# A token mixer's issue order: the forgetting norm's chain at high priority, a split traced behind the first casts, the stick-breaking sums bound two tiles on

## The chip, the cores and the metric

The kernel runs on one core of one Trainium2 chip. The metric is device time in microseconds (us) for one execution of the whole program; lower is better. Five engines run side by side, each with its own instruction stream, and meet only through semaphores: PE (TensorE, with its weight loads listed apart as PEld), DVE (VectorE), ACT (ScalarE), POOL (GpSimd) and SP (SyncE, which here only issues DMAs).

## The reference

A decoder trunk of two layers over 256 tokens of width 1024, in float32. Each layer is a feed-forward block (SwiGLU), a token mixer, and a second feed-forward block, each behind an RMS norm with a shift, a scale and a gate computed from a conditioning vector. The change lies in the mixer alone:

```python
def _mixer(h, w_in, ...):
    proj = h @ w_in
    (lru_x, lru_g, sb_q, sb_k, sb_v, fx_q, fx_k, fx_v, fx_f) = jnp.split(proj, SPLIT_POINTS, axis=-1)
    u = _causal_depthwise_conv(lru_x, conv_w, conv_b)
    y_lru = _rg_lru(u, ...) * jax.nn.gelu(lru_g)                   # recurrence
    y_sb = _stick_breaking_attention(sb_q, sb_k, sb_v)             # weights exp(log_beta + sums of log_1mb)
    fq, fk = _rms(fx_q) * g_qk[0], _rms(fx_k) * g_qk[1]            # the forgetting norm
    log_f = jax.nn.log_sigmoid(fx_f + b_fgate)
    y_fox = _forgetting_attention(fq, fk, fx_v, log_f)
    y = jnp.concatenate([_rms(y_lru), _rms(y_sb), _rms(y_fox)], axis=-1) * g_mix_out
    return y @ w_out
```

## The kernel before, in words

Tokens are two tiles of 128 rows (`t` = 0, 1). Every large weight arrives as a unit of 128x1024 float32 values (`raw`, six buffers), and is split into two parts that a fast matmul takes: `H`, a rounded copy made by ACT (L251), and `L`, the rest `raw - H`, made by DVE (L253). The activations are split in the same way into `hTh` and `hTl`, eight feature tiles of 128 each. A product is three matmuls: H with hTh, L with hTh, H with hTl.

The order of the instructions on each engine isn't written by hand. A scheduler places them at build time by a model of their times: whenever an engine comes free in its model, it takes, of the instructions whose inputs are ready, the one with the lowest priority number, which is the place in the program. Two constructs bend this. `with tc.high_priority()` gives what it holds the priority of the start of the program. `with tc.issue_after(ins)`, here often through the helper `behind(mul)`, lets what it traces on the engine of `ins` be queued only behind `ins`; on other engines it does nothing. On the chip every engine then runs its queue in that order, whatever is ready.

The mixer (`mixer`) goes through these steps, per layer:

- `proj(g, t)` multiplies the normed activations by the columns of group `g`: LG and LX (gate and input of the recurrence), FX (the forgetting q and k), then `proj_w(SB, b)` (stick-breaking q and k), then VV (both values). Each `proj` result lies in one of two PSUM banks (`PA`), so the third is not begun before the first is read out. `muls[g, t]` keeps the last matmul of each of the eight feature tiles; `muls[VV, 1][4]` is that of tile 4 of VV for the second token tile.
- Recurrence: four taps (L688, L691), the gates `go` (L698) with sigmoid and tanh, then, after `load_table("natural_log_exp_and_others")`, exponentials, a scan (L778) and the product with the gate (L831).
- The forgetting norm's chain, for each `t` (L726 to L734): square of the projection `o` on ACT (`fsq`), a sum over each head on DVE (`s8`), two logarithms and one exponential on ACT (`r8`), and the product `qa = o * r8` on DVE (L734), which is the last reader of the bank that holds `o`.
- Softmax of the forgetting attention, with its weights `p0`, `p1`; they are transposed later (L913) and copied to `pa`, `pb` (L914).
- The recurrence's group norm `group(hs, ...)` (L853 is its last product), and right behind it, at L861, `split(0, 4, hs)`: for each of four feature tiles one ACT instruction that writes `hTh` (L821) and one DVE instruction that reads it and writes `hTl` (L822).
- The stick-breaking weights, for two halves `e` = 0, 1: logits `zb`, `za` in PSUM; on ACT an absolute value, exponential and logarithm; on DVE L887; then casts on ACT (L893, `gh` and `ah`) and the remainders on DVE (L894, `gl` and `al`); then the sums, six matmuls onto `zb` and `za` (called through `more`, L231), at high priority and behind a tile of VV; then two exponentials (`wsb`, `wsa`).
- `values` (L925), the two remaining group norms and splits (feature tiles 6, 7 and 4, 5), and the output projection `w_out` (L264 to L266), whose first four feature tiles are the recurrence's. Then residual, the next norm (`xn`, L413) and its transposes (`tp`, L424), and the next feed-forward block (L277).

The helper that the change calls a second time is this:

```python
        def split(f0, n, src):
            for i in range(n):
                g = gm[:, f0 + i:f0 + i + 1]
                yh, yl = hTh[:, :, f0 + i, :], hTl[:, :, f0 + i, :]
                y = src[:, i, :].rearrange("p (t q) -> p t q", t=NT)
                A.activation(yh, y, AF.Copy, scale=g)
                V.scalar_tensor_tensor(out=yl, in0=y, scalar=g, in1=yh.bitcast(F32), ...)
```

Of the kernel before, what the change touches and what calls it, by code (L numbers as in the profile page):

```python
# [13 lines left out]
AF = mybir.ActivationFunctionType  # L14
ALU = mybir.AluOpType
AX = mybir.AxisListType
# [12 lines left out]
HD = 64  # L29
LX, LG, SB, FX, VV = range(5)  # L30
# [64 lines left out]
def trunk_kernel(ctx: ExitStack, tc: tile.TileContext, x, c, wst, ada, par, cst, row, wg, out):  # L95
# [14 lines left out]
    def W4(shape, dt=F32, name="w4"):  # L110
        return w4.tile(shape, dt, tag="w4", name=name)

    def W2(shape, dt=F32, name="w2"):
        return w2.tile(shape, dt, tag="w2", name=name)

    def SM(shape, dt=F32, name="sm"):
        return sm.tile(shape, dt, tag="sm", name=name)
# [4 lines left out]
    def PD(shape, name):  # L122
        return psd.tile(shape, F32, tag="d", name=name)

    def PT(shape, name):
        return pst.tile(shape, F32, tag="t", name=name)

    V, A, T, S = nc.vector, nc.scalar, nc.tensor, nc.sync
# [35 lines left out]
    def C(name):  # L164
        o, n = CST[name]
        return c_sb[:, o:o + n]

    def R(name):
        o, n = ROW[name]
        return r_sb[:, o:o + n]  # L170
# [7 lines left out]
    for n in range(2):  # L178
        q = slice(n * 512, (n + 1) * 512)
        o = PT([128, 512], name="pc")  # L180
# [5 lines left out]
    eps_t = const.tile([128, 1], F32, name="eps_t")  # L186
    V.memset(eps_t, EPS)
    eps64_t = const.tile([128, 1], F32, name="eps64_t")
# [41 lines left out]
    def more(o, **k):  # L230
        T.matmul(o, start=False, stop=True, skip_group_check=True, **k)  # L231
# [234 lines left out]
    def act(*a, **k):  # L466
        with tc.issue_after(table[-1].ins) if table else nullcontext():
            used.append(A.activation(*a, **k))  # L468
        return used[-1]
# [148 lines left out]
    def mixer(l, after):  # L618
# [7 lines left out]
        muls = {}  # L626

        def proj(g, t):
            o = PA([128, 512], name="pj")

            def w(k):
                q = slice((k % 2) * 512, (k % 2 + 1) * 512)
                if (g, t) == (LX, 0) and k == 2:
                    rooted.append(1)
                return [part[:, q] for part in unit(("in", l, g, k // 2))]

            muls[g, t] = over_features(o, t, w, (K_T[2], flush) if (g, t) == (LX, 0) else None, by=1)
            rooted.clear()
            ada_step(ADA_MIX[l] if g in (FX, VV) else 0)
            return o  # L640

        def proj_w(g, b):

            o = PA([128, 2, SEQ], name="pj")
            with ExitStack() as behind:
                for k in range(KT):
                    wh, wl = unit(("in", l, g, k // 2))
                    for h, w in ((0, wh), (0, wl), (1, wh)):
                        for i in range(2):
                            q = (k % 2) * 512 + (2 * b + i) * 128  # L650
                            opens = k == 0 and h == 0 and w is wh and i == 0
                            mul = T.matmul(o[:, i], lhsT=w[:, q:q + 128], rhs=(hTh, hTl)[h][:, :, k, :], start=opens,  # L652
                                           stop=True, skip_group_check=True)
                            if opens:
                                behind.enter_context(tc.issue_after(mul.ins))
            ada_step(ADA_MIX[l])
            return o

        def behind(mul):
            return tc.issue_after(mul.ins)  # L660
# [24 lines left out]
        if True:  # L685
            for f2, hf in enumerate(halves):
                for f in (2 * f2, 2 * f2 + 1):
                    A.activation(u[:, f, :], xT[:, f, 3:3 + SEQ], AF.Identity,  # L688
                                 scale=cw[:, 3 * 4 + f:3 * 4 + f + 1], bias=cbias[:, f:f + 1])
# [4 lines left out]
                for gi, (dst, b) in enumerate(((rg, P(f"br{l}")), (ig, P(f"bi{l}")))):  # L694
                    o = PD([128, 2, SEQ], name="go")
# [10 lines left out]
        qa = [const.tile([128, 8, 66], F32, name=f"qa{t}", tag=f"qa{t}") for t in range(NT)]  # L706
        for t in range(NT):
            o = proj(FX, t)
            if t == 1:
                z4 = SM([128, NT, 4], name="z4")  # L710
                fo = PT([8, NT, 128], name="fo")
                with tc.high_priority(), behind(muls[FX, 1][2]):
                    for k in range(KT):
                        T.matmul(fo, lhsT=wfs[:, k, :], rhs=hTh[:, :, k, :], start=k == 0, stop=False)
                        T.matmul(fo, lhsT=wfs[:, k, :], rhs=hTl[:, :, k, :], start=False, stop=k == KT - 1)
                zs = W2([8, NT, 128], name="zs")
                A.copy(zs, fo)
                zo = PT([128, NT, 4], name="zo")
                with behind(muls[FX, 1][7]):
                    for i in range(NT):  # L720
                        T.matmul(zo[:, i, :], lhsT=zs[:, i, :], rhs=C("fold")[0:8, :], start=True, stop=True)
                V.tensor_tensor(out=z4, in0=zo, in1=R(f"bf{l}").unsqueeze(1).to_broadcast([128, NT, 4]), op=ALU.add)
                z4 = z4.rearrange("p t h -> p (t h)")
            o3 = o.rearrange("p (h d) -> p h d", d=HD)
            sq = W2([128, 8, HD], name="fsq")
            A.activation(sq, o3, AF.Square)  # L726
            s8 = SM([128, 8], name="s8")
            V.tensor_reduce(out=s8, in_=sq, axis=AX.X, op=ALU.add)

            r8 = SM([128, 8], name="r8")  # L730
            act(r8[:, 0:4], s8[:, 0:4], AF.Ln, bias=eps64_t)
            act(r8[:, 4:8], s8[:, 4:8], AF.Ln, scale=1.0 / HD, bias=eps_t)
            act(r8, r8, AF.Exp, scale=-0.5)
            V.tensor_tensor(out=qa[t][:, :, 0:HD], in0=o3,  # L734
                            in1=r8.unsqueeze(2).to_broadcast([128, 8, HD]), op=ALU.mult)
            for i in range(2):
                V.tensor_tensor(out=qa[t][:, 4 * i:4 * i + 4, 0:HD], in0=qa[t][:, 4 * i:4 * i + 4, 0:HD],
                                in1=R(f"gqk{l}")[:, i * HD:(i + 1) * HD].unsqueeze(1).to_broadcast([128, 4, HD]),
                                op=ALU.mult)
            V.memset(qa[t][:, 0:4, 65:66], 1.0)  # L740
            V.memset(qa[t][:, 4:8, 64:65], 1.0)
# [26 lines left out]
        hs = W4([128, 4, SEQ], name="hs")  # L768
# [39 lines left out]
        for b in range(2):  # L808
            o = proj_w(SB, b)
# [6 lines left out]
# [6 lines that stand above are left out]
                V.scalar_tensor_tensor(out=yl, in0=y, scalar=g, in1=yh.bitcast(F32),  # L822
                                       op0=ALU.mult, op1=ALU.subtract)
# [58 lines left out]
        for e in range(2):  # L882
            for z, n in ((zb[e], nb[:, e]), (za[e], na[:, e])):
                A.activation(n, z, AF.Abs)
                act(n, n, AF.Exp, scale=-1.0)
                act(n, n, AF.Ln, bias=1.0)
                V.scalar_tensor_tensor(out=n, in0=z, scalar=0.0, in1=n, op0=ALU.max, op1=ALU.add)  # L887

            parts = []
            part_b = [gtp.tile([128, 2, 128], F32R, tag=n, name=n) for n in ("gh", "gl")]  # L890
            part_a = [W2([128, 2, SEQ], F32R, name=n) for n in ("ah", "al")]
            for n, (h, lo) in ((nb[:, e], part_b), (na[:, e], part_a)):
                A.copy(h, n)  # L893
                V.tensor_tensor(out=lo, in0=n, in1=h.bitcast(F32), op=ALU.subtract)  # L894
                parts.append((h, lo))
            with tc.high_priority(), behind(muls[VV, 1][(2, 6)[e]]):
                for i in range(2):
                    more(zb[e], lhsT=ntri_r, rhs=parts[0][i])
                    more(za[e][:, :, 128:256], lhsT=nones_r, rhs=parts[0][i])
                for i in range(2):  # L900
                    more(za[e], lhsT=ntri_r, rhs=parts[1][i])
            act(wsb[:, e], zb[e], AF.Exp)
            act(wsa[:, e], za[e], AF.Exp)
# [33 lines left out]
        o = {}  # L937
# [84 lines left out]
    for l in range(DEPTH):  # L1022
        ffn(l, 0, norm(l, 1), pre if l == 0 else {})
        mixer(l, norm(l, 2))
        ffn(l, 1, norm(l + 1, 0) if l + 1 < DEPTH else None)
# [94 lines left out]
```

## Time and profile before

| what | value |
|---|---|
| time, median of 3 runs | 994.08 us (993.16 to 994.2) |
| the profiled execution's own time | 993.75 us |
| its span, from the first to the last instruction | 992.0 us |
| granted TensorE clock | 1.000 |
| ACT busy | 531.6 us (54%) |
| DVE busy | 761.4 us (77%) |
| DMA moved | 251.26 MB, mean 253 GB/s |
| the mixers, roughly | 215 to 316 us and 701 to 800 us |

In the rows of the timeline the columns are start (us from the span's start), length, engine, line, operation, output<-inputs with their shapes, and how many in a row; a bracket gives the engine's idle time just ahead and what ended it. Instructions on one engine overlap at their ends, so that what a row costs its engine is the distance to the next start. A busy time of PE counts matmuls whose ends are modelled, so a PE that is shown busy all the time may still lose some tenths of a microsecond between two matmuls.

### The profile page before, as it was taken

What the parts mean: (1) busy time and instruction counts of PE and PEld (TensorE: products, weight loads), DVE (VectorE), ACT (ScalarE), POOL (GpSimd) and SP (SyncE); (2) the same over time, 40 slices, a digit from 0 to 9 for tenths busy, and PEclk for the clock granted to TensorE, in tenths of its full rate; (3) what the DMA queues carried; (4) which work ended last, traced back from release to release, by engine and by line L of the source; (5) the groups of instructions that cost most, each with busy time, mean ns of one, the idle gap of its engine ahead of it and who ended that gap; (6) DMA issues with size and microseconds to landing.
All of it is one profiled execution on the core that took longest, in us unless ns stands there. A gap on an engine that the chain in (4) does not pass through costs nothing.

```text
span 992.0 us, 15816 instructions
## 1 busy us (share of the span) xinstructions
PE 976.4 (98%) x6066; PEld 856.9 (86%) x6066; DVE 761.4 (77%) x1226; ACT 531.6 (54%) x854; POOL 6.9 (1%) x16
## 2 busy tenths in 40 slices
PE   6999999999999999999999999999999999999998
PEld 4999999877867899999888999997788778999996
DVE  8988888789996988888589888755877679646353
ACT  5374443577876444355465444455778765545340
POOL 0000000000000000000000000000000000000000
PEclk9999999999999999999999999999999999999999
DMA  8989999848672899999549999954652349745521
GB/s 316 362 325 344 350 336 341 304 169 322 210 251 71 302 393 347 305 335 342 200 148 345 367 351 338 329 173 155 206 176 86 107 129 356 286 163 198 185 65 42
DMA packets 70109, 251.26 MB, mean 253 GB/s; under 512 B 8081, under 2 KB 8977, under 8 KB 70034
## 3 DMA queue, kind: packets, MB, share of 16 engines
q1 hardware_dynamic: 68690, 246.83, 70.3%
q0 software_dynamic: 1056, 3.17, 0.9%
q8 instruction: 47, 0.77, 0.3%
q10 hardware_dynamic: 288, 0.26, 0.1%
q14 instruction: 28, 0.23, 0.1%
HBM read 249.16 MB, written 1.07 MB: 252 GB/s over the span
## 4 chain that ended last, share of the span: by engine, by line
PE 92%; DVE 3%; ACT 2%; DMA 1%; issue 0%; ACTq 0%; DVEq 0%; SPq 0%
PE up L476 39%; PE dn L266 8%; PE dn L264 8%; PE dn L265 8%; PE up L277 8%; PE pj L277 4%; PE up L279 4%; PE pj L279 2%; PE wo L264 1%; PE wo L265 1%; PE wo L266 1%; PE pj L652 1%; DVE L L253 1%; DMA raw<-in_wst 1%; PE go L698 1%; PE tp L424 1%
## 5 line engine op out<-in xcount | busy, mean ns | idle before, releaser
L253 DVE TENSOR_TENSOR L<-raw,H 128x1024 fp32r<-128x1024 f32 x320 | 381.0, 1220 | 70.1 <-ACT H L251 67.9
L251 ACT CAST H<-raw 128x1024 fp32r<-128x1024 f32 x320 | 328.4, 1050 | 85.5 <-DMA raw<-in_wst 40.1
L476 PE MATMUL up<-hTh,H 128*128 128x256 f32 x1088 | 211.0, 281 | 1.9 <-ACT H L251 1.9
L476 PE MATMUL up<-hTl,H 128*128 128x256 f32 x1088 | 209.8, 281 | 0.0
L476 PE MATMUL up<-hTh,L 128*128 128x256 f32 x1088 | 208.6, 279 | 0.0
L476 PEld LDWEIGHTS up<-hTh,H 128*128 128x128 f32 x1088 | 168.3, 189 | 8.5 <-ACT H L251 2.3
L476 PEld LDWEIGHTS up<-hTl,H 128*128 128x128 f32 x1088 | 164.0, 188 | 0.0
L476 PEld LDWEIGHTS up<-hTh,L 128*128 128x128 f32 x1088 | 163.2, 188 | 0.0
L468 ACT ACTIVATE sg<-up 128x256 f32<-128x256 f32 x88 | 33.9, 385 | 239.4 <-PE up L476 209.1
L264 PE MATMUL dn<-H,gh 128*128 128x512 f32 x344 | 136.5, 397 | 0.0
L266 PE MATMUL dn<-H,gl 128*128 128x512 f32 x344 | 136.5, 397 | 0.0
L265 PE MATMUL dn<-L,gh 128*128 128x512 f32 x344 | 135.6, 394 | 0.0
L298 DVE SCALAR_TENSOR_TENSOR raw<-raw,cb 128x1024 f32<-128x1024 f32 x96 | 114.1, 1218 | 0.0
L525 DVE TENSOR_TENSOR sg<-sg,up 128x256 f32<-128x256 f32 x68 | 28.4, 419 | 65.6 <-ACT sg L468 65.3
L266 PEld LDWEIGHTS dn<-H,gl 128*128 128x128 f32 x344 | 64.6, 188 | 15.4 <-DVE gl L542 0.5
L264 PEld LDWEIGHTS dn<-H,gh 128*128 128x128 f32 x344 | 64.6, 188 | 12.7 <-ACT gh L541 1.1
L265 PEld LDWEIGHTS dn<-L,gh 128*128 128x128 f32 x344 | 64.7, 188 | 12.3
L277 PE MATMUL up<-H,hTh 128*128 128x512 f32 x160 | 64.1, 401 | 0.6 <-DVE hTh L437 0.6
L277 PE MATMUL up<-L,hTh 128*128 128x512 f32 x160 | 63.6, 397 | 0.0
L279 PE MATMUL up<-H,hTl 128*128 128x512 f32 x160 | 57.7, 397 | 0.0
L323 DVE SCALAR_TENSOR_TENSOR raw<-raw,cb 128x1024 f32<-128x1024 f32 x48 | 56.7, 1218 | 0.7 <-DMA raw<-in_ada 0.7
L277 PE MATMUL pj<-H,hTh 128*128 128x512 f32 x128 | 52.3, 409 | 0.0
(237 smaller groups left out, 1065.7 us busy)
## 6 DMA issues: line engine op xcount, KB each, us to landing
raw<-in_wst SPq DMA_DIRECT2D x320, 512.0 KB, 5.3
raw<-in_ada SPq DMA_DIRECT2D x144, 512.0 KB, 5.5
gate<-row POOLq DMA_DIRECT2D x6, 512.0 KB, 7.4
x<-in_x SPq DMA_DIRECT2D x2, 512.0 KB, 4.2
wgt<-in_wg SPq DMA_DIRECT2D x2, 512.0 KB, 5.5
out_x<-x SPq DMA_DIRECT2D x3, 256.0 KB, 2.0
out_x<-x ACTq DMA_DIRECT2D x2, 128.0 KB, 1.7
once<-in_cst SPq DMA_DIRECT2D x1, 192.0 KB, 6.0
```

The source lines that it names most:

```text
L251: A.copy(h, raw)
L253: V.tensor_tensor(out=lo, in0=raw, in1=h.bitcast(F32), op=ALU.subtract)
L264: T.matmul(o, lhsT=xh, rhs=wh, start=first, stop=False)
L265: T.matmul(o, lhsT=xh, rhs=wl, start=False, stop=False)
L266: return T.matmul(o, lhsT=xl, rhs=wh, start=False, stop=last)
L277: T.matmul(o, lhsT=hh[:, k, :], rhs=part, start=k == 0 and i == 0, stop=False)
L279: mul = T.matmul(o, lhsT=hl[:, k, :], rhs=w(k)[0], start=False, stop=k == KT - 1)
L298: V.scalar_tensor_tensor(out=raw, in0=raw, scalar=1.0, in1=cb, op0=ALU.mult, op1=ALU.mult, accum_out=st[:, v, k:k + 1])
L323: V.scalar_tensor_tensor(out=raw, in0=raw, scalar=1.0, in1=cb, op0=ALU.mult, op1=ALU.mult, accum_out=col[:, k:k + 1])
L468: used.append(A.activation(*a, **k))
L476: return T.matmul(o[:, v], lhsT=w[:, q:q + 128], rhs=(hTh, hTl)[h][:, :, k, :], start=opens, stop=True, skip_group_check=True)
L525: V.tensor_tensor(out=sg, in0=sg, in1=o[:, 1], op=ALU.mult)
```

## The change

The forgetting norm's chain is put at high priority, for both token tiles. Inside the loop over `e`, for `e` = 0 and after its two casts, the recurrence's `split(0, 4, hs)` is traced, its ACT instructions behind the last of these casts. The sums are bound behind tile 4 (`e` = 0) and tile 7 (`e` = 1) of VV's second projection, where they were bound behind tiles 2 and 6. The call at L861 lies between the two hunks; no line of the diff touches it.

```diff
-            o3 = o.rearrange("p (h d) -> p h d", d=HD)
-            sq = W2([128, 8, HD], name="fsq")
-            A.activation(sq, o3, AF.Square)
-            s8 = SM([128, 8], name="s8")
-            V.tensor_reduce(out=s8, in_=sq, axis=AX.X, op=ALU.add)
-
-            r8 = SM([128, 8], name="r8")
-            act(r8[:, 0:4], s8[:, 0:4], AF.Ln, bias=eps64_t)
-            act(r8[:, 4:8], s8[:, 4:8], AF.Ln, scale=1.0 / HD, bias=eps_t)
-            act(r8, r8, AF.Exp, scale=-0.5)
-            V.tensor_tensor(out=qa[t][:, :, 0:HD], in0=o3,
-                            in1=r8.unsqueeze(2).to_broadcast([128, 8, HD]), op=ALU.mult)
+
+            with tc.high_priority():
+                o3 = o.rearrange("p (h d) -> p h d", d=HD)
+                sq = W2([128, 8, HD], name="fsq")
+                A.activation(sq, o3, AF.Square)
+                s8 = SM([128, 8], name="s8")
+                V.tensor_reduce(out=s8, in_=sq, axis=AX.X, op=ALU.add)
+
+                r8 = SM([128, 8], name="r8")
+                act(r8[:, 0:4], s8[:, 0:4], AF.Ln, bias=eps64_t)
+                act(r8[:, 4:8], s8[:, 4:8], AF.Ln, scale=1.0 / HD, bias=eps_t)
+                act(r8, r8, AF.Exp, scale=-0.5)
+                V.tensor_tensor(out=qa[t][:, :, 0:HD], in0=o3,
+                                in1=r8.unsqueeze(2).to_broadcast([128, 8, HD]), op=ALU.mult)
...
             for n, (h, lo) in ((nb[:, e], part_b), (na[:, e], part_a)):
-                A.copy(h, n)
+                cast = A.copy(h, n)
                 V.tensor_tensor(out=lo, in0=n, in1=h.bitcast(F32), op=ALU.subtract)
                 parts.append((h, lo))
-            with tc.high_priority(), behind(muls[VV, 1][(2, 6)[e]]):
+            if e == 0:
+
+                with tc.issue_after(cast.ins):
+                    split(0, 4, hs)
+            with tc.high_priority(), behind(muls[VV, 1][(4, 7)[e]]):
                 for i in range(2):
                     more(zb[e], lhsT=ntri_r, rhs=parts[0][i])
                     more(za[e][:, :, 128:256], lhsT=nones_r, rhs=parts[0][i])
```

## The prediction

> **What bounds the kernel.** I read the page first, then the waits of PE in each mixer, then the timeline of PE, ACT and DVE around each wait.
>
> ```profile
> span 992.0 us, 15816 instructions
> PE 976.4 (98%) x6066; PEld 856.9 (86%) x6066; DVE 761.4 (77%) x1226; ACT 531.6 (54%) x854; POOL 6.9 (1%) x16
> PE 92%; DVE 3%; ACT 2%; DMA 1%; issue 0%; ACTq 0%; DVEq 0%; SPq 0%
> ```
>
> PE is busy for 98% of the span and carries 92% of the chain that ended last. The change adds and removes no matmul. So it can act only through the moments in which PE, which takes its queue in order, stands at an instruction whose input is late. In the first mixer (215 to 325 us) the waits of PE that bear on the change are two:
>
> ```profile
> PE zb L231 <- ACT gh L893: 1.0, 1, 1.0
> PE pj L652 <- DVE qa L734: 0.9, 1, 0.9
> ```
>
> The second mixer has neither: from 705 to 812 us the longest wait in PE's list is this one, at a place that the diff leaves alone:
>
> ```profile
> PE up L277 <- DVE hTh L437: 0.3, 1, 0.3
> ```
>
> So even a change that did all it could at these two places would win 1.9 us of 993.75, the profiled execution's own time (1.75 us of which lie outside the span). That is 0.2%, and 0.2% is also about what a measurement of this kernel can tell from no change: 2 us either way.
>
> **Part one: the forgetting norm's chain.** The second wait above ends at the product `qa`. Here are ACT, then DVE, then PE of the first mixer, and behind them ACT of the second at the same point.
>
> ```profile
> 245.78 1.28 ACT L463 ACT_TABLE_LOAD   x1
> 247.08 0.49 ACT L468 ACTIVATE r<-s,eps_t 128x4 f32<-128x4 f32 x2
> 247.47 1.04 ACT L251 CAST H<-raw 128x1024 fp32r<-128x1024 f32 x1
> 248.41 0.20 ACT L468 ACTIVATE r<-r 128x8 f32<-128x8 f32 x1
> ```
>
> ```profile
> 241.44 0.68 DVE L728 TENSOR_REDUCE s<-fsq 128x8 f32<-128x512 f32 x1
> 248.83 0.17 DVE L722 TENSOR_TENSOR z<-zo,r_sb 128x8 f32<-128x8 f32 x1 [0.41 <-PE zo L721]
> 248.91 0.68 DVE L734 TENSOR_TENSOR qa<-pj,r 128x512 f32<-128x512 f32 x1
> ```
>
> ```profile
> 249.74 0.47 PE L652 MATMUL pj<-hTh,H 128*128 128x256 f32 x2 [0.95 <-DVE qa L734]
> ```
>
> ```profile
> 730.69 0.49 ACT L468 ACTIVATE r<-s,eps_t 128x4 f32<-128x4 f32 x2
> 731.09 1.03 ACT L251 CAST H<-raw 128x1024 fp32r<-128x1024 f32 x1
> 732.02 0.20 ACT L468 ACTIVATE r<-r 128x8 f32<-128x8 f32 x1
> ```
>
> Square and sum are done by 242.12 (241.44 + 0.68), and the logarithms start only when the table is loaded, at 247.08. Nothing that brings these two forward helps. What is left is the cast of 0.94 us (247.47 to 248.41) between logarithms and exponential, and the addition `z` of 0.08 us (248.83 to 248.91) ahead of `qa`. The cast belongs to a weight of a later group, so the exponential had the better place in the program already, and the scheduler still put the cast first, in both layers. A rule of priorities explains that only if the exponential wasn't ready, in the scheduler's model, when ACT came free: it needs the logarithms' result. A still better priority doesn't make it ready. So I take the cast to stay and only `z` to give way: **-0.1 us**, in the first layer; in the second there is no wait to win.
>
> The bounds: if the exponential does go ahead of the cast, all of the wait of 0.95 us goes. On the other side, the reduction (0.68 us on DVE) may now be queued ahead of the recurrence's taps and products, and the square ahead of sigmoids. Whoever waits for those (the gates `go` on PE, and behind them the table load) could come 0.68 us later. Part one is thus -0.95 to +0.7, and I take the value near zero, because the two rows of casts speak for it. No DMA and no queue of SP or POOL is moved.
>
> **Part two: the split.** The title says that the recurrence's split now stands behind the first casts. The diff adds it there and removes nothing: its second hunk is displaced by the same two lines as the first leaves, so L861 stays and the split is issued twice. Values don't change, since the same numbers are written again. What one split costs, and where it stands in the first layer, on ACT and then on DVE:
>
> ```profile
> L821 ACT ACTIVATE hTh<-hs,p_sb x8: 492/494/511, 282.4 to 767.5; 128x256 fp32r<-128x256 f32 x8
> ```
>
> ```profile
> 282.37 1.71 ACT L821 ACTIVATE hTh<-hs,p_sb 128x256 fp32r<-128x256 f32 x4 [1.42 <-DVE hs L853]
> 283.98 0.39 ACT L893 CAST gh<-nb 128x256 fp32r<-128x256 f32 x1
> 284.79 0.58 ACT L859 COPY vt<-pj 128x512 f32<-128x512 f32 x1
> 285.27 0.42 ACT L468 ACTIVATE nb<-nb 128x256 f32<-128x256 f32 x1
> ```
>
> ```profile
> 283.19 1.66 DVE L822 SCALAR_TENSOR_TENSOR hTl<-hs,p_sb,hTh 128x256 fp32r<-128x256 f32 x4
> 285.10 0.68 DVE L894 TENSOR_TENSOR al<-na,ah 128x512 fp32r<-128x512 f32 x1
> ```
>
> So the change adds 1.71 us on ACT and 1.66 us on DVE per layer, 16 instructions over both layers. The cast `gh` still stands behind the first split, and the wait of 1.0 us for it stays. What is new is that `w_out` of the recurrence's four tiles must wait for the second write of `hTh` and `hTl`. PE in the first layer, before:
>
> ```profile
> 282.93 0.51 PE L264 MATMUL wo<-H,hTh 128*128 128x512 f32 x1
> 284.42 0.38 PE L231 MATMUL zb<-gh,ntri_r 128*128 128x256 f32 x1 [0.99 <-ACT gh L893]
> 284.76 0.39 PE L265 MATMUL wo<-L,hTh 128*128 128x512 f32 x1
> 284.99 0.40 PE L266 MATMUL wo<-H,hTl 128*128 128x512 f32 x1
> 285.81 0.40 PE L264 MATMUL wo<-H,hTh 128*128 128x512 f32 x1
> ```
>
> One such matmul costs PE 0.23 us (284.76 to 284.99). Up to 285.81 PE has started four of them around the sums (282.93, 284.76, 284.99, 285.81). After the change the first tile is rewritten on ACT at 284.79 (behind the casts, where now `vt` stands) or, if `vt` goes first, at 285.27, and is there 0.49 us later, at 285.28 or 285.76. The slot at 285.81 is the first that can serve, and its `hTl` follows when DVE is through with `al` (285.78) and one remainder (a quarter of 1.66, 0.42), at 286.20. So with the slot of 285.81 PE has started one of the four and lacks three: 3 x 0.23 = **+0.7 us**. The second layer, ACT and then PE:
>
> ```profile
> 768.68 0.41 ACT L468 ACTIVATE nb<-nb 128x256 f32<-128x256 f32 x1
> ```
>
> ```profile
> 768.42 0.28 PE L231 MATMUL zb<-gh,ntri_r 128*128 128x256 f32 x1
> 768.66 0.39 PE L279 MATMUL pj<-H,hTl 128*128 128x512 f32 x1
> 768.89 0.39 PE L264 MATMUL wo<-H,hTh 128*128 128x512 f32 x1
> 769.68 0.40 PE L265 MATMUL wo<-L,hTh 128*128 128x512 f32 x1
> ```
>
> Here the first tile is back at 768.68 + 0.49 = 769.17. The matmul of 768.89 can't run then, but the slot of 769.68 can serve; one matmul is lost, **+0.2 us**.
>
> Behind the second split, in ACT's queue, stand the other half's logarithms and casts, the exponentials of the first half and the copies of the transposed softmax weights; on DVE, the other half's remainders. All come up to 1.7 us later. PE has other `w_out` matmuls to run meanwhile, those of the second token tile, and the end of the mixer has room. ACT's last step of the next norm and PE's transposes of it, in the first layer and then in the second:
>
> ```profile
> 310.39 1.34 ACT L413 ACTIVATE xn<-x,ny 128x512 f32<-128x512 f32 x2 [1.53 <-DVE ny L370]
> 794.35 1.34 ACT L413 ACTIVATE xn<-x,ny 128x512 f32<-128x512 f32 x2 [1.53 <-DVE ny L370]
> ```
>
> ```profile
> 313.19 1.04 PE L424 MATMUL tp<-c_sb,xn 128*128 128x128 f32 x8
> 797.61 1.04 PE L424 MATMUL tp<-c_sb,xn 128*128 128x128 f32 x8
> ```
>
> `xn` is ready at 311.73 and PE comes to it at 313.19: 1.46 us of room; in the second layer 795.69 against 797.61, 1.92 us. With PE itself 0.7 and 0.2 us later the room is 2.1 us in both, more than 1.7. So I cost this at **nothing**, as long as the matmuls of the second token tile fill in; without that cover it is the rival below.
>
> **Part three: the sums.** In the first layer the first half's sums run at 284.42, behind VV's last matmul; in the second at 768.42, inside tile 7, whose last matmul is the L279 of 768.66. Both lie past tile 4 already, and the other half's stand behind `w_out` matmuls. New bounds at tiles 4 and 7 don't bind: **0**. If they did, a half's sums could come one tile (three matmuls, 0.7 us) later on a queue that has other matmuls to run.
>
> The sum is -0.1 + 0.7 + 0.2 + 0 = +0.8 us: 994.55 us for an execution like the profiled one, and 994.9 by the median, which lies 0.33 above it.
>
> **The rivals.** *The exponential goes ahead of the cast.* For it: the chain now ranks with the start of the program. Against it: the two casts that overtook a better-placed exponential. It gives 0.85 us more, so the change about cancels: 994.1.
>
> *Slower: ACT's second split is passed on whole.* The mechanism is PE's fixed order: the other half's sums and the values stand among the `w_out` matmuls where the scheduler's model puts them, and if ACT arrives late there, PE waits although other matmuls are ready behind. The price is bounded by how little ACT can absorb. Busy times by stretch; the columns are stretch, length, then PE, PEld, DVE, ACT and POOL, and the granted clock:
>
> ```profile
> 282.80:292.00 9.20, 8.17 (x47) 5.36 (x46) 9.20 (x18) 8.91 (x21) 0.00 (x0) 1.00 0.62 228
> 768.80:780.00 11.20, 11.20 (x68) 7.47 (x67) 7.19 (x11) 10.37 (x19) 0.00 (x0) 1.00 0.28 86
> ```
>
> ACT idles 0.29 and 0.83 us in them, so 1.42 + 0.88 = 2.3 us come through, or twice 1.71 = 3.4 if none of the idle time lies in the right place; less 0.1, this is 996.3 to 997.4. It decides once what stands in PE's queue ahead of the other half's sums ends before their casts, which now come 1.7 us later. For it: DVE is busy for all of the first stretch, so the remainders can't catch up there. Against it: the scheduler knows of the second split, and orders PE's queue with it.
>
> *Faster: the casts land ahead of the first split, too.* With new times in its model the scheduler may put `gh` where ACT idled 1.42 us for `hs`. If the exponential goes ahead as well, and PE finds enough ready matmuls to cover the second split, the 1.0 and the 0.95 us both go: 992.1. That takes three things at once, and the first isn't asked for by the diff.
>
> *The clock falls.* In the stretch from 282.8 to 292, PE has 1.03 us without a matmul and the granted clock stays 1.00. A longer gap, as `w_out` now leaves one before the sums, could make the array start slow again: if the matmuls of a stretch of 3.4 us ran at half rate, that would cost 1.7 us a layer and 998.3 in all. The Trainium skill, in "TensorE: Matmul & The Clock Gate", section "What's actually happening", says that the clock halves after about 3.4 us of idleness and comes back after as long a busy time. By that rule gaps of 1 to 2 us leave the clock alone, and the trace agrees as far as its 1.03 us goes.
>
> **How the numbers follow.** Chances: forecast 0.47; exponential first 0.15; second split passed on 0.28; casts ahead of both 0.08; clock 0.02. Forecast and first rival lie within 2 us of the median; so the chances are 0.62 for no change, 0.30 for slower and 0.08 for faster. The time is the forecast's, 994.9. The range runs from 993.0, the forecast with part one at its lower bound and about a microsecond of reordering in its favour, to 997.4, the upper end of the slower rival. It leaves out the faster rival, the clock, and little else.
>
> **What would show it.** Right: L821 for `hs` counts 16 and not 8, and L822 as well; the first `w_out` matmul stands behind the first half's sums in the first layer; PE still waits about 1 us for `gh`; a cast still stands between logarithms and exponential; the sums lie past tile 4. Wrong: no PE wait for `qa` (part one), new PE waits for `wsa`, `ah` or `pa` (the slower rival), `gh` ahead of L821, or a granted clock under 1.00 in either mixer.

## The result, and the profile after

The changed kernel takes 1001.39 us (median of 4 runs, 999.94 to 1002.1) against 993.97 us (4 runs, 993.16 to 994.2): 1.0077 times as long, with a 95% interval of 1.0065 to 1.0089. It is 7.4 us slower, and outside the forecast range. The profiled execution took 1001.25 us, with a span of 999.2. The page and PE's waits from 240 to 330 us:

```profile
span 999.2 us, 15837 instructions
PE 980.0 (98%) x6066; PEld 860.7 (86%) x6066; DVE 765.8 (77%) x1234; ACT 535.4 (54%) x862; POOL 6.9 (1%) x16
PE 91%; DVE 5%; ACT 2%; DMA 1%; issue 1%; DVEq 0%; ACTq 0%
```

```profile
PE pj L652 <- DVE qa L736: 2.7, 1, 2.7
PE zb L231 <- ACT gh L895: 2.5, 1, 2.5
PE zb L231 <- DVE gl L896: 0.4, 1, 0.4
```

ACT and DVE have 8 instructions more: the second split. The two waits of before are still there, at the same two places, but they come to 5.6 us with the new one for `gl`, where they were 1.9. That is 3.7 of the 7.2 us that the span has grown. The rest shows in no list of waits, because PE is busy in it. Stretches of the changed kernel; the third column from the end is the granted clock:

```profile
250.00:252.00 2.00, 0.84 (x4) 0.87 (x5) 2.00 (x3) 1.03 (x6) 0.00 (x0) 0.56 1.00 389
252.00:254.00 2.00, 2.00 (x11) 2.00 (x11) 2.00 (x7) 0.12 (x1) 0.00 (x0) 0.50 1.04 410
254.00:256.00 2.00, 2.00 (x12) 2.00 (x11) 1.32 (x4) 1.78 (x2) 0.00 (x0) 0.50 0.70 266
292.00:294.00 2.00, 2.00 (x6) 1.57 (x5) 2.00 (x6) 1.55 (x5) 0.00 (x0) 0.50 0.53 188
```

Behind each of the two waits the matmuls run at half clock. In PE's timeline behind the first wait, two matmuls take 0.43 us (251.73 to 252.16), where before they took 0.235:

```profile
247.88 0.60 PE L721 MATMUL zo<-c_sb,zs 8*128 8x4 f32 x4
251.16 0.77 PE L652 MATMUL pj<-hTh,H 128*128 128x256 f32 x2 [2.68 <-DVE qa L736]
251.73 0.63 PE L652 MATMUL pj<-hTh,L 128*128 128x256 f32 x2
252.16 0.63 PE L652 MATMUL pj<-hTl,H 128*128 128x256 f32 x2
257.06 0.28 PE L751 MATMUL fp<-lf,c_sb 128*128 128x8 f32 x2
```

With such landmarks on PE the difference can be laid out. Each column is the distance between the starts of two rows of matmuls of the same place in the program: `zo`, the first of the projection behind it (L652), `fp`, then the next block's first `up` (L277) in the first layer and in the second. The first wait lies in the first column, the second in the third. The rows below "after" are the experiments.

| kernel | `zo` to projection | projection to `fp` | `fp` to `up` | `up` to second `up` |
|---|---|---|---|---|
| before | 1.55 | 3.26 | 62.91 | 484.42 |
| after | 3.28 | 5.90 | 65.62 | 484.84 |
| e1, high priority alone | 3.28 | 4.62 | 62.90 | 484.35 |
| e2, second split alone | 1.55 | 3.26 | 65.27 | 484.81 |
| e3, split moved | 1.55 | 3.26 | 63.62 | 484.36 |
| e4, split moved, high priority | 3.29 | 5.89 | 63.74 | 484.14 |
| e5, high priority, no tie | 1.55 | 3.26 | 62.75 | 484.43 |
| e6, after, ten fillers | 3.29 | 3.16 | 65.72 | 484.80 |
| e7, after, twice ten fillers | 3.29 | 3.15 | 64.66 | 484.80 |
| e8, split moved, bounds 7 and 7 | 1.56 | 3.25 | 62.72 | 484.10 |
| e9, after, five fillers | 3.28 | 3.26 | 65.60 | 484.78 |
| e10, after, no tie | 1.55 | 3.26 | 64.87 | 484.54 |

After less before: 1.73 + 2.64 + 2.71 + 0.42 = 7.5 us. `zo` itself comes 0.3 us sooner (247.88 against 248.19), which leaves the 7.2 of the span. The first column is the longer wait, the second the clock, and the third has both.

Why is `qa` late? ACT of the changed kernel, then DVE:

```profile
246.73 0.49 ACT L468 ACTIVATE r<-s,eps_t 128x4 f32<-128x4 f32 x2
247.12 1.04 ACT L251 CAST H<-raw 128x1024 fp32r<-128x1024 f32 x1
248.07 0.58 ACT L728 ACTIVATE fsq<-pj 128x512 f32<-128x512 f32 x1
248.55 0.20 ACT L468 ACTIVATE r<-r 128x8 f32<-128x8 f32 x1
```

```profile
248.52 0.17 DVE L722 TENSOR_TENSOR z<-zo,r_sb 128x8 f32<-128x8 f32 x1 [0.25 <-PE zo L721]
248.60 1.22 DVE L253 TENSOR_TENSOR L<-raw,H 128x1024 fp32r<-128x1024 f32 x1
249.74 0.68 DVE L730 TENSOR_REDUCE s<-fsq 128x8 f32<-128x512 f32 x1
250.34 0.68 DVE L736 TENSOR_TENSOR qa<-pj,r 128x512 f32<-128x512 f32 x1
```

The cast still stands between logarithms and exponential, and `z` still ahead of `qa`. New is that the second token tile's square (`fsq`) stands ahead of the first tile's exponential, and its sum (`s`), with one `L` (L253) besides, ahead of the first tile's `qa`. On DVE that is 1.14 + 0.60 = 1.74 us: the whole of the first column.

The theory taken to the experiments (A): both tiles' chains now have the priority of the program's start, so the scheduler has nothing left that puts the first ahead of the second; the tie makes `qa` late, and idle times of more than 2 us let the clock fall. The rival (B): the second split is the cost, and the rest follows from it. The priority numbers of the built program make A's first half more exact: each `with tc.high_priority()` block counts from 0 again, so that the second tile's square has the number 0 and the first tile's exponential 4. The square outranks the exponential; it does not merely tie with it. The word "tie" stands below for this inversion.

### The profile page after: what moved, and what is told of

Its sections match the earlier page's. It is cut to its first block, busy times and chain, and to the rows that moved or that the text cites. A ratio compares the mean times of both kernels' runs of the same rounds, so it can differ in the third digit from the quotient of the medians.

```text
span 999.2 us, 15837 instructions
## 1 busy us (share of the span) xinstructions
PE 980.0 (98%) x6066; PEld 860.7 (86%) x6066; DVE 765.8 (77%) x1234; ACT 535.4 (54%) x862; POOL 6.9 (1%) x16
## 4 chain that ended last, share of the span: by engine, by line
PE 91%; DVE 5%; ACT 2%; DMA 1%; issue 1%; DVEq 0%; ACTq 0%
PE up L476 39%; PE dn L266 8%; PE dn L264 8%; PE dn L265 8%; PE up L277 8%; PE up L279 4%; PE pj L277 4%; PE pj L652 2%; PE pj L279 2%; PE wo L264 1%; PE wo L266 1%; PE wo L265 1%; DVE L L253 1%; DVE raw L298 1%; PE go L698 1%
## 5 line engine op out<-in xcount | busy, mean ns | idle before, releaser
L253 DVE TENSOR_TENSOR L<-raw,H 128x1024 fp32r<-128x1024 f32 x320 | 381.6, 1221 | 73.3 <-ACT H L251 72.0
L298 DVE SCALAR_TENSOR_TENSOR raw<-raw,cb 128x1024 f32<-128x1024 f32 x96 | 114.1, 1221 | 0.2 <-DMA raw<-in_ada 0.2
L277 PE MATMUL up<-H,hTh 128*128 128x512 f32 x160 | 64.1, 401 | 0.5 <-DVE hTh L437 0.5
L277 PE MATMUL up<-L,hTh 128*128 128x512 f32 x160 | 63.6, 397 | 0.0
L277 PE MATMUL pj<-H,hTh 128*128 128x512 f32 x128 | 52.3, 409 | 0.0
```

The source lines that it names most:

```text
L253: V.tensor_tensor(out=lo, in0=raw, in1=h.bitcast(F32), op=ALU.subtract)
L277: T.matmul(o, lhsT=hh[:, k, :], rhs=part, start=k == 0 and i == 0, stop=False)
L298: V.scalar_tensor_tensor(out=raw, in0=raw, scalar=1.0, in1=cb, op0=ALU.mult, op1=ALU.mult, accum_out=st[:, v, k:k + 1])
```

## The experiments

**e1, high priority alone, and e2, the second split alone** (with the new bounds; with the bounds alone the program builds to the same queue on every engine as before, so that they do nothing without the rest). e1 has the first hunk only, e2 this:

```diff
-                A.copy(h, n)
+                cast = A.copy(h, n)
...
+            if e == 0:
+                with tc.issue_after(cast.ins):
+                    split(0, 4, hs)
-            with tc.high_priority(), behind(muls[VV, 1][(2, 6)[e]]):
+            with tc.high_priority(), behind(muls[VV, 1][(4, 7)[e]]):
```

> The kernel before with the high priority alone. Theory A (a tie at equal priority): the second token tile's square and reduction now overtake the first tile's exponential and product, PE waits about 2.7 us for that product in the first layer instead of 0.9, and the granted clock then falls to about 0.5 for some 6 us; 1.7 us of wait and 2.6 us of slow matmuls, less 0.3 us gained ahead of it, makes 998.0 (+4.0), and a profile with a stretch of clock near 0.5 behind 250 us. Theory B (the second split is what costs): the high priority is neutral, 993.9 within 1 us, and no wait for qa over 1 us.

> The kernel before with the second split and the new bounds, without the high priority. Theory A: the rest of the loss, 7.4 - 4.0 = 3.4 us at most; of this about 1.5 us is direct (w_out's first tile must wait for the second write of hTh) and 1.7 us a stretch of half clock that may or may not come: 995.5 to 997.4. Theory B: nearly the whole loss, 1000 to 1001.

e1: 996.63 us, ratio 1.0035 (1.0022 to 1.0048). e2: 996.51, ratio 1.0030 (1.0019 to 1.0042). They cost 3.2 and 3.1 us, so that neither is the whole, and together they make 6.3 of the 7.4 us. The wait of 2.7 us for `qa` and the fall of the clock behind it belong to the high priority (first two columns); the second split has a fall of its own, behind its wait for `gh`. PE of e1 shows the slow stretch with both of its ends:

```profile
251.68 0.47 PE L652 MATMUL pj<-hTh,H 128*128 128x256 f32 x2 [2.68 <-DVE qa L736]
252.90 0.40 PE L652 MATMUL pj<-hTl,H 128*128 128x256 f32 x2
253.52 0.63 PE L652 MATMUL pj<-hTh,L 128*128 128x256 f32 x2
253.95 0.63 PE L652 MATMUL pj<-hTl,H 128*128 128x256 f32 x2
256.08 0.41 PE L652 MATMUL pj<-hTh,L 128*128 128x256 f32 x1
```

The idle time is the same 2.68 us as in the changed kernel, but the matmuls start at full rate, turn slow 1.4 us later, and are fast again 3.4 us after that. That is why the same wait costs 1.4 us of clock here and 2.6 there, and why e1 stayed below the 998.0 expected.

**e3, the split moved** as the title says (the call at L861 removed), without high priority, and **e4**, the same with it:

```diff
-        split(0, 4, hs)
```

> The kernel before with the split really moved: the call behind the group norm is taken out, the one behind the first casts and the new bounds stay; no high priority. Theory A: the wait of 1.0 us for gh in the first layer goes, nothing is issued twice: 993.0 (-1.0), bounds 992.4 to 994.0. Theory B, by which the position behind the casts is harmful in itself because w_out's first tile comes later: 994.5 to 996.

> The changed kernel with the first split taken out, so that the split is moved and not issued twice; with the high priority. Theory A: the loss of the high priority stays and that of the second issue goes: 997 (+3), with a wait of about 2.7 us for qa in the first layer. Theory B: all the loss goes, 993 to 994.

e3: 994.35, ratio 1.0010 (1.0001 to 1.0020), a miss: a gain was expected. PE's waits in e3:

```profile
PE zb L231 <- ACT gh L892: 1.4, 1, 1.4
PE pj L652 <- DVE qa L734: 0.9, 1, 0.9
```

The wait for `gh` has grown instead of going: with `gh` early in the scheduler's model, the sums were put at 283.40, ahead of VV's last tiles (last matmul at 285.18), and PE stood at them with VV matmuls ready behind. e4: 997.59, ratio 1.0040 (1.0025 to 1.0054); the wait for `qa` is 2.7 us again and the clock falls behind it. So high priority costs 3.2 us in either setting.

**e5, the tie undone.** High priority as in e1, but the second tile's square and sum are queued behind the first tile's exponential and `qa`:

```diff
-                A.activation(sq, o3, AF.Square)
+                with behind(chain[0]) if t else nullcontext():
+                    A.activation(sq, o3, AF.Square)
...
-                V.tensor_reduce(out=s8, in_=sq, axis=AX.X, op=ALU.add)
+                with behind(chain[1]) if t else nullcontext():
+                    V.tensor_reduce(out=s8, in_=sq, axis=AX.X, op=ALU.add)
...
+                chain = [act(r8, r8, AF.Exp, scale=-0.5),
+                         V.tensor_tensor(out=qa[t][:, :, 0:HD], in0=o3, ...)]
```

> High priority for the forgetting norm's chain alone (no second split, the sums bound as before), with the tie between the two token tiles undone: on ACT the second tile's square is queued behind the first tile's exponential, on DVE the second tile's sum is queued behind the first tile's qa. Theory A (the tie made qa late, and the late qa let the clock fall): the wait for qa is back at 0.9 to 1.0 us, the granted clock from 250 to 258 us is 1.00, and the time is 993.3 to 994.0 where high priority alone took 996.6. Theory B (high priority costs by what it moves elsewhere, the tie is an accident beside it): the time stays at 996 or more. If the exponential should go ahead of the cast, which neither expects, the wait would be gone and the time 992.5 to 993.

993.76, ratio 1.0000 (0.9991 to 1.0010): all that high priority cost is gone. DVE of e5:

```profile
249.33 0.17 DVE L722 TENSOR_TENSOR z<-zo,r_sb 128x8 f32<-128x8 f32 x1 [0.26 <-PE zo L721]
249.42 0.68 DVE L738 TENSOR_TENSOR qa<-pj,r 128x512 f32<-128x512 f32 x1
250.01 0.68 DVE L732 TENSOR_REDUCE s<-fsq 128x8 f32<-128x512 f32 x1
```

`qa` follows `z` again, the wait is 0.9 us, and the clock stays at 1.00. High priority without the tie is worth nothing: the cast ahead of the exponential stays.

**e6 and e7, the idle time filled.** The changed kernel, with ten matmuls that nobody reads behind `zo` in the first layer (e6), and ten more behind VV's last matmul (e7). They need neither ACT nor DVE:

```diff
+                if l == 0:
+                    dm = PT([128, 512], name="dm")
+                    with tc.high_priority(), behind(zmul):
+                        for i in range(10):
+                            T.matmul(dm, lhsT=idb, rhs=mask[:, 0:1, :].to_broadcast([128, 4, 128]), start=True, stop=True)
```

> The changed kernel plus ten matmuls whose result nobody reads, in the first layer, right behind zo in PE's queue, where PE otherwise stands 2.7 us and waits for qa. They need no work of another engine. Theory A (the length of PE's idle time lowered the clock): the projection behind still starts at about 251.2 us, but its matmuls run at full rate, the granted clock from 250 to 258 is 0.95 to 1.00, the first layer's end comes 2.6 us earlier, and the time is 998.5 to 999.2 where the change took 1001.4. Rival B (the matmuls of 251 to 257 us are slow because of their weights or of what DMA moves then, and the clock is no cause): they stay at 0.43 us each, and the time is 1001 to 1002.

> As the run with ten filling matmuls before the projection, and ten more in the first layer behind VV's last matmul, where PE otherwise waits for gh for 2.5 us. Theory A: the granted clock from 288 to 296 us is 0.95 to 1.00 as well, and the time is another 1.7 us lower, 996.8 to 997.6; what is left over the kernel before is 1.4 to 1.7 us of wait at qa, 1.5 us at gh, and some tenths in the second layer. Rival B: no lower than the run with the first filling alone, within 0.5 us.

e6: 998.86, ratio 1.0050 (1.0033 to 1.0066), by the medians 2.5 us less than the changed kernel, though its four runs spread from 997.1 to 1000.07. Its PE:

```profile
249.90 2.33 PE L726 MATMUL dm<-mask,idb 128*128 128x512 bf16 x10
252.65 0.47 PE L652 MATMUL pj<-hTh,H 128*128 128x256 f32 x2 [0.42 <-DVE qa L741]
252.95 0.39 PE L652 MATMUL pj<-hTh,L 128*128 128x256 f32 x2
253.18 0.39 PE L652 MATMUL pj<-hTl,H 128*128 128x256 f32 x2
```

The projection starts as late as before the filling (3.29 us behind `zo`), on the same operands, and runs at full rate: 3.16 us to `fp` instead of 5.90. So the slow matmuls come from PE's idle time and from nothing else that changed. e7: 997.82, ratio 1.0042 (1.0027 to 1.0057), another 1.0 us and not the 1.7 expected. The ranges of e6 and e7 overlap, so that this rests more on the third column, which is 1.06 us shorter. The clock is 1.00 behind the second wait too; three of the ten fillers ran only behind the wait, at 0.23 us each, and take back up to 0.7.

**e8, the moved split with both sums behind tile 7**, no high priority: e3 with one number changed.

```diff
-            with tc.high_priority(), behind(muls[VV, 1][(4, 7)[e]]):
+            with tc.high_priority(), behind(muls[VV, 1][(7, 7)[e]]):
```

> The recurrence's split moved as the title says (the call at L861 removed), no high priority, and the sums of both halves bound behind tile 7 of VV's second projection instead of 4 and 7, so that PE does not stand at them with VV matmuls behind. Theory A (the 0.9 us that the moved split lost with bounds 4 and 7 are sums placed before their casts): the wait for gh is at most 0.5 us and the time 993.0 to 993.6, as the kernel before or up to 1 us better. Theory B (moving the split is no gain whatever the bound, since the matmuls of w_out that it feeds are then late in its place): the time is 994 to 994.6 as with bounds 4 and 7, the wait being for hTh in place of gh.

993.29, ratio 0.9998 (0.9988 to 1.0007). The loss of e3 is gone, so that it lay in the place of the sums. But there is no gain either, though the wait for `gh` is down from 1.0 to 0.2 us. PE at the first sum, and a weight load of `w_out` behind it:

```profile
282.89 0.39 PE L231 MATMUL zb<-gh,ntri_r 128*128 128x256 f32 x1 [0.22 <-ACT gh L892]
284.99 0.19 PEld L264 LDWEIGHTS wo<-H,hTh 128*128 128x128 f32 x1 [0.57 <-ACT vt L859]
```

From the first sum to `up` it is 32.7 us (282.89 to 315.60), and it was 31.5 (284.42 to 315.91). The `w_out` matmuls that filled PE before now wait for ACT themselves: the weight load of the first one 0.2 us for `hTh` of its own split, and that at 284.99 for the copy `vt`, which ACT makes between the second and the third tile of the split (0.57 us for the load, a hole of 0.3 us between the matmuls). The wait was not removed but spread.

**e9, half the filling:** e6 with five fillers.

> The changed kernel plus five filling matmuls behind zo in the first layer, so that PE stands idle for about 1.6 us of the 2.7 before the projection. It asks how long an idle time has to be to lower the clock. Theory A1 (an idle time well over 1 us is enough, as the run with the split alone, 1.5 us at gh, already suggests): the granted clock from 250 to 258 us stays at or below 0.9 and the time is 1000 to 1001.4. Theory A2 (it takes 2.5 us or more): the clock is 0.98 to 1.00 and the time 998.5 to 999.2, as with ten.

999.04, ratio 1.0050 (1.0037 to 1.0064). PE:

```profile
251.88 0.47 PE L652 MATMUL pj<-hTh,H 128*128 128x256 f32 x2 [1.50 <-DVE qa L741]
252.20 0.40 PE L652 MATMUL pj<-hTh,L 128*128 128x256 f32 x2
```

1.5 us of idle time did not lower the clock here, which is not yet a limit, since e2's 1.48 us did (see the last section); behind the 2.5 us at `gh`, which was left alone, it fell as in the changed kernel.

**e10, the changed kernel without the tie** (the edit of e5 in the whole change).

> The changed kernel whole, except that the tie between the two token tiles is undone as in the run with high priority alone. Theory A (the tie and the second split cost independently of each other): the wait for qa is back at 0.9 to 1.0 us, the wait for gh stays at 1.4 to 2.5, and the time is 996.4 to 997.3, as with the second split alone. Rival (the gap at gh in the changed kernel is longer, 2.5 against 1.5 us, because the projection came late): the same wait for qa, but gh at 1.5 us and the clock behind it no lower than 0.85, time 995.8 to 996.5.

995.61, ratio 1.0018 (1.0009 to 1.0028): over the kernel before this is 1.8 us, so that the tie is worth some 5.6 of the 7.4, more than the 3.2 of e1. It came out below the 996.4 of Theory A and just below the 995.8 of its rival, whose waits it has. Its waits, then the start of the recurrence's last product `hs` on its DVE:

```profile
PE zb L231 <- ACT gh L897: 1.5, 1, 1.5
PE pj L652 <- DVE qa L738: 0.9, 1, 0.9
```

```profile
280.79 1.23 DVE L298 SCALAR_TENSOR_TENSOR raw<-raw,cb 128x1024 f32<-128x1024 f32 x1
281.94 1.22 DVE L857 TENSOR_TENSOR hs<-hs,rl 128x1024 f32<-128x1024 f32 x1
```

And DVE of the changed kernel at that place:

```profile
283.27 1.23 DVE L298 SCALAR_TENSOR_TENSOR raw<-raw,cb 128x1024 f32<-128x1024 f32 x1
284.42 1.23 DVE L298 SCALAR_TENSOR_TENSOR raw<-raw,cb 128x1024 f32<-128x1024 f32 x1
285.56 1.23 DVE L855 TENSOR_TENSOR hs<-hs,rl 128x1024 f32<-128x1024 f32 x1
```

In the plan with the tie, four L298 stand ahead of `hs`, from 280.99 on; without it two. ACT waits for `hs` before it splits and casts. Measured from VV's last matmul (286.44, and 283.34 in e10), `hs` starts 0.5 us later, which is half of the difference at the sums. The other half is on ACT of the changed kernel, where the copy `vt` stands inside the first split, ahead of the cast `gh`, and costs 0.47 us (288.04 to 288.51); in e10 it stands behind the casts:

```profile
288.04 0.56 ACT L861 COPY vt<-pj 128x512 f32<-128x512 f32 x1
288.51 0.51 ACT L823 ACTIVATE hTh<-hs,p_sb 128x256 fp32r<-128x256 f32 x1
```

So the wait at the sums is 2.5 us and not 1.5, and the clock falls there a second time.

**e11, the cast put behind the exponential**, on e8: the weight cast that stands between them is queued behind the first tile's exponential.

> The moved split with both sums behind tile 7, as before, and in addition the weight cast that stands on ACT between the forgetting norm's logarithms and its exponential is queued behind the exponential, for both layers. This also moves other casts of the scheduler's plan. Theory A (the two waits are all that the two places hold, and both can go): the wait for qa falls from 0.9 to at most 0.2 us and the time is 992.0 to 992.8. Rival (the cast that gives way is late for the projection behind it, or the plan that follows loses as much elsewhere): a new wait for H of 0.5 us or more, and 993.0 to 994.0.

996.65, ratio 1.0029 (1.0019 to 1.0040), above both expectations. The wait for `qa` is gone from the first mixer, and others come for it:

```profile
PE za L231 <- ACT ah L896: 1.3, 1, 1.3
PE zb L231 <- ACT gh L896: 0.6, 1, 0.6
```

The plan changed in many places, so that this says only that the 0.9 us at `qa` is not to be had by this edit. Which of the new places costs the rest was not separated. No version here beats the kernel before by more than its interval.

## Why the prediction was wrong

**Part one, the step that failed.** "So I take the cast to stay and only `z` to give way: -0.1 us." The cast stayed, as forecast from the two rows, and `z` kept its place, too. The step asked what the chain would overtake and did not ask what would overtake it now. Each token tile's chain was raised by itself, so that the second tile's square and sum went ahead of the first tile's exponential and `qa`. The bound of part one did name the sum (0.68 us on DVE), but with the recurrence as its victim; with the L253 that went along it was 1.74 us, at `qa` itself, over twice the bound of +0.7. That this order is what costs is shown by e5 and e10, which turn it round and change nothing else by hand.

**The clock, the second step that failed.** "By that rule gaps of 1 to 2 us leave the clock alone" rested on 1.03 us of idle time in one stretch and on a sentence that the prediction drew from the Trainium skill ("TensorE: Matmul & The Clock Gate", section "What's actually happening"). The late `qa` and the second split brought idle times of 2.7 and 2.5 us, and the clock fell behind both; in e2 it fell behind 1.5 us, inside what the sentence called safe. It cost 2.64 us behind `qa` (second column; with the wait filled, in e6, it is 3.16 again) and 1.0 to 1.7 behind `gh` (e7, without and with its three late fillers). This rival had a chance of 0.02 and a price of 1.7 us a layer; it came twice in one layer. The mechanism was on the list, its condition wasn't tied to the bounds of the other parts.

**Part two, the right mechanism, mis-sized.** "3 x 0.23 = +0.7 us" for the first layer, +0.2 for the second. e10, where the clock stays at 1.00, shows 1.96 (64.87 less 62.91) and 0.12, and 1.8 us of time. Some 0.5 of the 1.96 lies ahead of VV's last matmul (29.99 us from `fp` to it, and 29.48 before); 0.4 of that is a wait of `tf` for `qaT`, which neither e2 nor e5 has, so that it is not the split's by itself. The split's share in the first layer is thus about 1.45 us, twice the forecast. Behind VV's last matmul, the first `w_out` matmul starts at 287.00 in e10, so that PE lacks four of them around the sums and not three (0.9 us); it waits 0.3 us for `gl`, which `w_out` matmuls had covered, and 0.3 ahead of the first matmul with the rewritten `hTl`. The room at the next norm did hide ACT's delay: no new wait appears at `tp` or `up`, and the first split's 2.3 to 3.4 us of the slower rival did not come through. The sign of that rival was right, its reason only in small part.

**Part three held:** the new bounds alone do not bind; the program built with them has the same queues. They do once the split is really moved (e3), and then to the worse.

**What would show it:** L823 (L821 before) for `hs` counts 16, the first `w_out` matmul stands behind the sums, the cast stays. Against it stood "PE still waits about 1 us for `gh`" (2.5), and the granted clock under 1.00, which the prediction had listed as a sign that it was wrong.

## What to carry to other kernels

Raising a chain that exists once per tile, each copy by itself, puts the younger copy's first steps ahead of the older one's last; bind the copies behind one another (e5), or try raising only the first, which no run here did. When a step moves what PE waits for, price the idle time twice: its length, and, once it may pass some 1.7 us, a stretch or two of 3.4 us at about half rate behind it (here 1.4 and 2.6 us). And a wait removed where the work behind it hangs on the same engine is spread and not won (e8).

## What the runs showed of the hardware

PE's granted clock fell to 0.50 behind idle times well under the length that was expected. Of the profiled executions, it fell behind all three waits of 2.68 us for `qa` (after, e1, e4) and all three of 2.5 us for `gh` (after, e6, e9). At 1.5 us it fell in one (e2) and not in two others (e9 at `qa`, and e10 at `gh`, where PE's idle time is the same as e2's within 0.04 us). At 0.9 to 1.4 us it never fell. PE in e2, where it did:

```profile
284.69 0.39 PE L231 MATMUL zb<-gh,ntri_r 128*128 128x256 f32 x1 [1.48 <-ACT gh L893]
285.51 0.58 PE L231 MATMUL zb<-gl,ntri_r 128*128 128x256 f32 x1 [0.31 <-DVE gl L894]
```

The traces show what sets these apart. Within a trace the changes of the granted clock lie whole multiples of 3.41 us apart (in the changed kernel at 250.22, 257.05, 291.18 and 294.60 us), and the grid lies elsewhere in every traced execution. Where a mixer has no change, the grid is counted on from the last one before it (in e10 from 22.14 us). What counts is the idle time that falls into one stretch of this grid. Two stretches of e2, then two of e10; the columns are stretch, length, then the busy time of PE, PEld, DVE, ACT and POOL (with the number of instructions), the granted clock, the DMA share and GB/s:

```profile
282.07:285.49 3.42, 1.65 (x7) 0.86 (x5) 3.42 (x9) 2.85 (x7) 0.00 (x0) 1.00 0.95 376
285.49:288.90 3.41, 3.39 (x9) 2.81 (x10) 3.41 (x8) 3.41 (x10) 0.00 (x0) 0.50 0.23 90
281.55:284.96 3.41, 2.18 (x10) 1.42 (x8) 3.41 (x8) 2.01 (x6) 0.00 (x0) 1.00 0.90 291
284.96:288.37 3.41, 2.70 (x11) 1.75 (x12) 3.41 (x8) 3.41 (x9) 0.00 (x0) 1.00 0.56 228
```

In e2 the waits for `gh` and `gl` leave PE idle for 1.77 us of one stretch, and the next is at half clock. In e10 a border cuts the same wait in two, 1.23 us of idle time fall into the one stretch and 0.71 into the other, and the clock stays. Over all 13 traces, every stretch of a mixer at full clock with 1.72 to 2.16 us idle (seven) was followed by one at half clock, and none with 1.26 us or less was; where between the two the limit lies was not measured. In the changed kernel and e4 the first slow stretch still held 0.94 and 0.97 us of the wait for `qa`, and a second slow one followed, 6.83 us in all; in e1 it held none, and 3.41 us was all. So the price of the same wait is a matter of luck: of e1's five executions and e4's five, one each had a mean granted clock of 1.000, which leaves no room for even one slow stretch, and these were e4's fastest at 996.31 and e1's at 996.02 us.

The Trainium skill, in "TensorE: Matmul & The Clock Gate", section "What's actually happening", has a window of about 3.4 us that runs freely and doesn't start with the work; the grid of 3.41 us agrees with that. It also has the throttled state come after at least one idle window of that length; by that, 2.5 us would have been safe, and here the measurement decides: 1.72 us idle in one window were enough.
